# An RWKV-7 operand stage rewritten: scan over the raw tanh, key scale inside other operations, one factor on ScalarE

## The chip, the cores and the metric

The kernel runs on 1 core of a Trainium2 chip. The metric is the device time of one launch in microseconds (us), from runs of the same program; the time before is the median of 3 runs.

Engines are named as in the profile: PE (TensorE matmul), PEld (its weight load), DVE (VectorE), ACT (ScalarE), POOL (GpSimd), SP (SyncE, which issues most DMAs). Each works through its own instructions in order and waits for the others by semaphores.

## The reference, cut to what matters

A decoder trunk of two layers on 1024 tokens of width 1024. Layer 0 is an S5 diagonal SSM beside differential attention; layer 1 is RWKV-7 time mixing with 16 heads of 64; each is followed by a SwiGLU FFN of 2816 hidden columns. The change touches the operands of the RWKV-7 recurrence only:

```python
w = -softplus(-(w0 + tanh(xw @ w1) @ w2)) - 0.5
decay = exp(-exp(w))
k = xk @ w_k
a = sigmoid(a0 + (xa @ a1) @ a2)                 # learning rate, one per channel
kk = k * k_k
kk = kk / max(sqrt(sum(kk * kk, per head)), 1e-12)
k = k * (1.0 + (a - 1.0) * k_a)
# state: S_t = S_{t-1} diag(decay_t) + (S_{t-1} (-kk_t)) (kk_t*a_t)^T + v_t k_t^T;  y_t = S_t r_t
```

With a sigmoid written as 0.5 + 0.5 tanh(x/2), the log of the decay is -0.5 e^-0.5 (1 + tanh), and a is 0.5 (1 + tanh).

## The kernel before, in words

Dense products run on PE as three matmuls each (high and low parts of operands and weights, line 466), 128x512 a piece. Every weight block is loaded by DMA, rounded by ACT (`whi`, line 449) and its remainder taken by DVE or, in the stretches below, by POOL (`wlo`, line 450).

The recurrence is done in blocks of 512 tokens (two), each with 16 units: 8 pairs of heads times 2 pieces of 256 tokens. `rwkv_algebra` runs 19 steps per block. In a step four generators advance in lockstep on four successive units: `rwkv_prep` (operands, lines 1429 to 1496), `rwkv_inv` (a triangular inverse, built up in five rounds of small matmuls, lines 1566 to 1625), `rwkv_rec` (the recurrence over four chunks of 64 tokens, lines 1649 to 1676) and `rwkv_out`. Between their yields the matmuls of a dense product (FFN or projection) are woven in, so PE has work while the small chains pass through other engines. The order of PE's instructions is the order of the program text (`manual_schedule` for PE alone); the order on DVE, ACT, POOL and SP is set by a scheduler when the program is built.

Per unit `rwkv_prep` makes on [128 x 256] tiles: the log decay `lwt` (tanh on ACT, an affine on DVE, line 1430), its running sum `L` (four scans of 64, line 1432), `Wx` and `Wi` (exp of L and of -L, ACT), the learning rate `at` (tanh on ACT, affine on DVE, line 1445), the scaled key `kr` (DVE, 1447) and its square (ACT), the inverse root per head (`head_rsqrt`, which ends in a PE product `hbc`), then `kk` (DVE, 1453), `bt` (POOL, 1455, in the tile named `ksq`), the key factor `fk` (DVE, 1457, in the tile named `kr`), `k2` (DVE, 1459, in the tile named `lwt`), the four quarters of `FS` (bt and k2 times Wi, line 1464), and `AR` (kk times Wx on 1468, r times Wx on 1469). POOL makes `RV` = r times k2 (1470) and `FE` (1545).

In `rwkv_rec` each chunk is a chain of PE and DVE: PE `pR` (1649), DVE copy `Pb` (1655), PE `pR` (1659), copies `XU` (ACT 1660, DVE 1661), PE `pR` (1665), DVE state update `XH` (1672), and PE 1649 of the next chunk.

Of the kernel before, what the change touches and what calls it, by code (L numbers as in the profile page):

```python
# [12 lines left out]
AF = mybir.ActivationFunctionType  # L13
ALU = mybir.AluOpType
# [4 lines left out]
P = 128  # L19
# [18 lines left out]
EXPMH = math.exp(-0.5)  # L38
# [108 lines left out]
class Trunk:  # L147
# [1100 lines left out]
    def proj_open(self):  # L1248
        nc = self.nc
        v = nc.vector  # L1250
        vp = self.vp = self.open("m1v", 1)
        self.lastc = vp.tile([P, KT, 1], F32, name="m1lc")
        nc.gpsimd.memset(self.lastc, 0.0)
        vec = self.vec = vp.tile([P, 4, 8], F32, name="m1vec")
        o = self.v2
        v.tensor_scalar(vec[:, 0, :], self.vc2[:, o["od_w0"] : o["od_w0"] + 8], 0.5, None, op0=ALU.mult)
        v.tensor_scalar(vec[:, 1, :], self.vc2[:, o["od_a0"] : o["od_a0"] + 8], 0.5, None, op0=ALU.mult)
        v.tensor_scalar(vec[:, 2, :], self.vc2[:, o["od_k_a"] : o["od_k_a"] + 8], -1.0, 1.0, op0=ALU.mult, op1=ALU.add)
        self.omu = vp.tile([P, 48], F32, name="omu")
        v.tensor_scalar(self.omu, self.vc2[:, o["od_mu"] : o["od_mu"] + 48], -1.0, 1.0, op0=ALU.mult, op1=ALU.add)  # L1260

        self.tw, self.ta = (vp.tile([P, TB], F32, name=f"lt{i}") for i in "wa")
        nc.gpsimd.memset(self.tw[64:128, :], 0.0)
        nc.gpsimd.memset(self.ta[0:64, :], 0.0)
        self.sg = vp.tile([P, TB], F32, name="lsg")
        self.kd = self.dr.tile([3, 8, P, S], F32, name="kd")
        self.zd = self.dr.tile([8, P, S], F32, name="zd")
# [132 lines left out]
    def rwkv_prep(self, q, j, st):  # L1400


        nc = self.nc
        ap, pr, vec = self.ap, self.pr, self.vec
        v, g_, s_ = nc.vector, nc.gpsimd, nc.scalar
        sl = slice(j * P, (j + 1) * P)
        tok = slice(q * TR, (q + 1) * TR)
        tw, ta = (a[:, (q * TR) % TB : (q * TR) % TB + TR] for a in (self.tw, self.ta))
        M = ALU.mult
        rows = (slice(0, 64), slice(64, 128))  # L1410

        def t(tag, bufs=1, shape=None):
            return ap.tile(shape or [P, TR], F32, tag=tag, name=self.nm(tag), bufs=bufs)

        def c8(a):
            return a.rearrange("p (c t) -> p c t", t=64)

        ks, rr, RV = t("ks", 2), t("rr", 2), t("RV", 4, [P, 2, TR])
        for d, dst in ((0, ks), (1, rr), (2, RV[:, 1, :])):
            nc.sync.dma_start(dst, self.kd[d, j][:, tok])  # L1420
        wa2 = t("wa2", 2, [P, P])
        nc.sync.dma_start(wa2[0:64, :], self.A["od_w2"][0][:, sl])
        nc.sync.dma_start(wa2[64:128, :], self.A["od_a2"][0][:, sl])
        pz = pr.tile([P, TR], F32, tag="k", name=self.nm("pz"))
        nc.tensor.matmul(pz, lhsT=wa2, rhs=tw, start=True, stop=True)
        yield

        lwt, L = t("lwt"), t("L")
        s_.activation(lwt, pz, AF.Tanh, bias=vec[:, 0, j : j + 1], scale=0.5)
        v.tensor_scalar(lwt, lwt, -0.5 * EXPMH, -0.5 * EXPMH, op0=M, op1=ALU.add)  # L1430
        for c in range(0, TR, 64):
            v.tensor_tensor_scan(
                L[:, c : c + 64], self.ones[:, 0:1].to_broadcast([P, 64]), lwt[:, c : c + 64], 0.0, op0=M, op1=ALU.add
            )
        Wx = t("Wx", 1, [P, CR, 65])
        g_.memset(Wx[:, :, 0:1], 1.0)
        s_.activation(Wx[:, :, 1:65], c8(L), AF.Exp)
        Wi = L
        s_.activation(Wi, L, AF.Exp, scale=-1.0)
        pa = pr.tile([P, TR], F32, tag="k", name=self.nm("pa"))  # L1440
        nc.tensor.matmul(pa, lhsT=wa2, rhs=ta, start=True, stop=True)
        yield
        at = t("at")
        s_.activation(at, pa, AF.Tanh, bias=vec[:, 1, j : j + 1], scale=0.5)
        v.tensor_scalar(at, at, 0.5, 0.5, op0=M, op1=ALU.add)
        kr, ksq = t("kr"), t("ksq")
        v.tensor_scalar(kr, ks, self.col("od_k_k", j), None, op0=M)
        s_.activation(ksq, kr, AF.Square)
        yield
        rn = yield from self.head_rsqrt(ap, pr, "k", ksq, 1.0, None, 1e-24, TR // P)  # L1450
        yield
        kk = t("kk")
        v.tensor_tensor(kk, kr, rn, op=M)
        bt = t("ksq")
        g_.tensor_tensor(bt, kk, at, op=M)
        fk = t("kr")
        v.tensor_scalar(fk, at, self.col("od_k_a", j), vec[:, 2, j : j + 1], op0=M, op1=ALU.add)  # L1457
        k2 = t("lwt")
        v.tensor_tensor(k2, ks, fk, op=M)
        FS = t("FS", 2, [P, CR, P])  # L1460
        for h in range(2):
            r = rows[h]
            for x, o in ((bt, 64 * h), (k2, 64 - 64 * h)):
                v.tensor_tensor(FS[r, :, o : o + 64], c8(x)[r], c8(Wi)[r], op=M)  # L1464
        AR = [t(f"AR{h}", 3, [P, CR, P]) for h in range(2)]
        for h in range(2):
            r = rows[h]
            v.scalar_tensor_tensor(AR[h][r, :, 0:64], c8(kk)[r], -1.0, Wx[r, :, 0:64], op0=M, op1=M)  # L1468
            v.tensor_tensor(AR[h][r, :, 64:128], c8(rr)[r], Wx[r, :, 1:65], op=M)
        g_.tensor_tensor(RV[:, 0, :], rr, k2, op=M)  # L1470
        wc = t("wc", 3, [P, CR])
        g_.tensor_copy(wc, Wx[:, :, 64])
        st["pre"] = AR, FS, RV, wc
        yield

        XH, XU = ([t(f"{k}{h}", 3, [P, CR, 64]) for h in range(2)] for k in ("XH", "XU"))
        pv = pr.tile([P, CR, 64], F32, tag="k", name=self.nm("pv"))
        for c in range(CR):
            for h in range(2):
                nc.tensor.matmul(  # L1480
                    pv[rows[1 - h], c, :], lhsT=RV[rows[h], 1, c * 64 : (c + 1) * 64], rhs=self.cst("cen")[rows[h]], start=True, stop=True
                )
        for h in range(2):
            s_.copy(XH[h][rows[1 - h]], pv[rows[1 - h]])
            s_.copy(XU[h][rows[1 - h]], pv[rows[1 - h]])
        yield

        AB = t("AB", 3, [P, CR, P])
        msk = self.cst("tri").rearrange("p (o n) -> p o n", o=1)
        pas = [pr.tile([P, CR, P], F32, tag=g, name=self.nm("pA")) for g in "ky"]  # L1490
        for c in range(CR):
            for h in range(2):
                nc.tensor.matmul(pas[h][:, c, :], lhsT=FS[rows[h], c, :], rhs=AR[h][rows[h], c, :], start=True, stop=True)  # L1493
        for h, pa in enumerate(pas):
            for r, dst in ((rows[h], AB), (rows[1 - h], AR[h])):
                v.tensor_tensor(dst[r], pa[r], msk[r].to_broadcast([64, CR, P]), op=M)
            yield
        st["val"] = XH, XU, AB
# [364 lines left out]
```

## Time and profile before

| | |
|---|---|
| median of 3 runs | 3262.19 us (3261.68 to 3269.7) |
| profiled execution, its own time | 3254.43 us |
| its span in the trace | 3252.6 us |
| PE busy | 3020.0 us, 93% of the span |
| DVE busy | 1988.2 us, 61% |
| ACT busy | 1135.6 us, 35% |
| POOL busy | 913.8 us, 28% |
| mean granted TensorE clock | 0.964 |

A busy share is an average over stages with different limits. The two recurrence blocks lie at about 1190 to 1790 us and 2090 to 2690 us of the span. The profiled execution is one run of the program; it lies 7.8 us below the median of the runs. A granted clock of 1.00 is 2.4 GHz, one of 0.50 is 1.2 GHz.

### The profile page before, as it was taken

The page shows a single profiled execution, that of the slowest core. Times are in us where ns is not written, and L with a number is a line of the kernel's source. Part 1 is how long each engine was busy: PE and PEld are TensorE (multiplying, and loading weights), DVE is VectorE, ACT ScalarE, POOL GpSimd, SP SyncE. Part 2 cuts the span into 40 slices and gives each one's busy share as a digit, 9 for nine tenths or more (in the row PEclk, how much of TensorE's full clock was granted, in tenths as well). Part 3 has the DMA queues.
Part 4 walks back from the last instruction along what each step waited for, and adds up shares of the span by engine and source line. Part 5 has one row for each costly group of instructions (what it writes and reads, how often), then busy time and mean ns, then how long its engine had stood idle before and what let it go on. Part 6 is the DMA issues. An engine that isn't in the chain of part 4 may idle for free. (4 is left out here: it accounts for less than half of the span.)

```text
span 3252.6 us, 52003 instructions
## 1 busy us (share of the span) xinstructions
PE 3020.0 (93%) x19966; PEld 2255.1 (69%) x19966; DVE 1988.2 (61%) x4013; ACT 1135.6 (35%) x2286; POOL 913.8 (28%) x1034
## 2 busy tenths in 40 slices
PE   5789999998999999999899999999999999999999
PEld 2678866776777676666666776666666667777777
DVE  7754655556665556777777456467777774444443
ACT  3212443333224543333333246433333332322222
POOL 6643310001103103443433441034434334300000
PEclk7889998999999999999999999999999999999999
DMA  7753221226555441221221254422212212533333
GB/s 250 220 118 68 72 79 46 80 72 194 183 167 162 142 137 58 66 74 58 79 66 55 80 171 130 149 61 68 74 53 83 69 53 80 170 89 93 97 101 94
DMA packets 489864, 338.47 MB, mean 104 GB/s; under 512 B 44280, under 2 KB 451088, under 8 KB 488592
## 3 DMA queue, kind: packets, MB, share of 16 engines
q1 hardware_dynamic: 474288, 304.75, 31.2%
q0 software_dynamic: 7632, 25.64, 2.5%
q10 hardware_dynamic: 7696, 4.74, 0.6%
q8 instruction: 159, 2.61, 0.3%
q14 instruction: 89, 0.73, 0.1%
HBM read 292.59 MB, written 42.47 MB: 103 GB/s over the span
## 5 line engine op out<-in xcount | busy, mean ns | idle before, releaser
L449 ACT CAST whi<-wraw 128x1024 fp32r<-128x1024 f32 (+2 forms) x472 | 401.8, 852 | 896.3 <-PE pd L466 186.4
L466 PE MATMUL pd<-dd,whi 128*128 128x512 f32 x1408 | 464.0, 411 | 16.3 <-DVE x L534 12.2
L450 POOL TENSOR_TENSOR wlo<-wraw,whi 128x1024 fp32r<-128x1024 f32 (+2 forms) x184 | 326.6, 1776 | 483.1 <-ACT whi L449 403.1
L450 DVE TENSOR_TENSOR wlo<-wraw,whi 128x1024 fp32r<-128x1024 f32 (+2 forms) x288 | 297.4, 1033 | 264.0 <-ACT whi L449 252.3
L466 PE MATMUL pg<-fhi,whi 128*128 128x512 f32 x704 | 304.9, 433 | 13.2 <-DVE sg L521 10.8
L466 PEld LDWEIGHTS pd<-dd,whi 128*128 128x128 f32 x1408 | 253.4, 189 | 83.3 <-ACT whi L449 16.3
L466 PE MATMUL pu<-fhi,whi 128*128 128x512 f32 x704 | 298.8, 424 | 1.3 <-ACT ev L1359 0.6
L466 PE MATMUL pg<-fhi,wlo 128*128 128x512 f32 x704 | 284.9, 405 | 6.3 <-DVE wlo L450 6.3
L466 PE MATMUL pu<-fhi,wlo 128*128 128x512 f32 x704 | 281.6, 400 | 4.0 <-POOL wlo L450 2.4
L466 PE MATMUL pg<-flo,whi 128*128 128x512 f32 x704 | 283.4, 403 | 0.0
L466 PE MATMUL pd<-dd,wlo 128*128 128x512 f32 x704 | 279.2, 397 | 2.6 <-DVE wlo L450 2.1
L466 PE MATMUL pu<-flo,whi 128*128 128x512 f32 x704 | 280.8, 399 | 0.0
L534 DVE SCALAR_TENSOR_TENSOR x<-pd,mod,x 128x512 f32<-128x512 f32 x192 | 143.4, 747 | 125.3 <-PE pd L466 124.3
L466 PE MATMUL pkrv<-xh,whi 128*128 128x512 f32 x384 | 163.7, 426 | 12.5 <-ACT ev L1359 6.8
L466 PEld LDWEIGHTS pg<-fhi,whi 128*128 128x128 f32 x704 | 136.4, 194 | 49.0 <-DVE sg L521 11.9
L466 PEld LDWEIGHTS pg<-fhi,wlo 128*128 128x128 f32 x704 | 136.2, 193 | 40.6 <-DVE wlo L450 8.7
L466 PEld LDWEIGHTS pd<-dd,wlo 128*128 128x128 f32 x704 | 133.2, 189 | 39.2 <-DVE wlo L450 6.4
L466 PEld LDWEIGHTS pu<-fhi,whi 128*128 128x128 f32 x704 | 133.9, 190 | 37.8 <-issue 3.0
L466 PEld LDWEIGHTS pu<-fhi,wlo 128*128 128x128 f32 x704 | 134.5, 191 | 36.6 <-POOL wlo L450 3.3
L466 PE MATMUL pkrv<-xh,wlo 128*128 128x512 f32 x384 | 153.2, 399 | 2.5 <-DVE wlo L450 2.5
L466 PEld LDWEIGHTS pg<-flo,whi 128*128 128x128 f32 x704 | 137.0, 195 | 25.4
L466 PEld LDWEIGHTS pu<-flo,whi 128*128 128x128 f32 x704 | 134.9, 192 | 25.7
(459 smaller groups left out, 6116.0 us busy)
## 6 DMA issues: line engine op xcount, KB each, us to landing
wraw<-in_ffn_w_gate SPq DMA_DIRECT2D x88, 512.0 KB, 3.8
wraw<-in_ffn_w_up SPq DMA_DIRECT2D x88, 512.0 KB, 3.8
wraw<-in_ffn_w_down SPq DMA_DIRECT2D x128, 256.0 KB, 2.6
mwt<-in_w_ada POOLq DMA_DIRECT2D x48, 512.0 KB, 5.3
mwt<-in_w_ada SPq DMA_DIRECT2D x32, 512.0 KB, 5.8
wraw<-in_ffn_w_down SPq DMA_DIRECT2D x64, 192.0 KB, 2.3
kd<-ev SPq DMA_DIRECT2D x48, 256.0 KB, 2.0
xs<-x SPq DMA_DIRECT2D x8, 1024.0 KB, 5.6
```

The costliest lines, as they stand in the source:

```text
L449: nc.scalar.copy(hi, raw)
L450: (eng or nc.vector).tensor_tensor(lo, raw, hi.bitcast(F32), op=ALU.subtract)
L466: nc.tensor.matmul(out, lhsT=w(k), rhs=x(k), start=first and i == 0, stop=last and i == n - 1)
L534: nc.vector.scalar_tensor_tensor(x[:, n, :], pd, gate[:, n : n + 1], x[:, n, :], op0=ALU.mult, op1=ALU.add)
```

## The change

What it does, per unit of `rwkv_prep` (one more column group of constants, 0.5 k_a, is made once in `proj_open`):

- The affine on `lwt` goes. The scan's first operation becomes an add of the ones, so it sums 1 + tanh; the factor -0.5 e^-0.5 moves into the scale of the two exps.
- The affine on `at` goes: `at` stays the raw tanh. `bt` becomes (at + 1) times kk, on DVE (it was on POOL), and the missing 0.5 is put into the product with Wi (`FS`), which becomes a SCALAR_TENSOR_TENSOR.
- `kr` = k times k_k goes: the square takes k_k as ACT's scale, `kk` takes it as the scalar of a SCALAR_TENSOR_TENSOR.
- `fk` moves from DVE to ACT, with scale 0.5 k_a and bias 1 - 0.5 k_a.

```diff
@@ -1255,7 +1255,8 @@
         o = self.v2
         v.tensor_scalar(vec[:, 0, :], self.vc2[:, o["od_w0"] : o["od_w0"] + 8], 0.5, None, op0=ALU.mult)
         v.tensor_scalar(vec[:, 1, :], self.vc2[:, o["od_a0"] : o["od_a0"] + 8], 0.5, None, op0=ALU.mult)
-        v.tensor_scalar(vec[:, 2, :], self.vc2[:, o["od_k_a"] : o["od_k_a"] + 8], -1.0, 1.0, op0=ALU.mult, op1=ALU.add)
+        v.tensor_scalar(vec[:, 2, :], self.vc2[:, o["od_k_a"] : o["od_k_a"] + 8], -0.5, 1.0, op0=ALU.mult, op1=ALU.add)
+        v.tensor_scalar(vec[:, 3, :], self.vc2[:, o["od_k_a"] : o["od_k_a"] + 8], 0.5, None, op0=ALU.mult)
         self.omu = vp.tile([P, 48], F32, name="omu")
         v.tensor_scalar(self.omu, self.vc2[:, o["od_mu"] : o["od_mu"] + 48], -1.0, 1.0, op0=ALU.mult, op1=ALU.add)
 
@@ -1427,41 +1428,39 @@
 
         lwt, L = t("lwt"), t("L")
         s_.activation(lwt, pz, AF.Tanh, bias=vec[:, 0, j : j + 1], scale=0.5)
-        v.tensor_scalar(lwt, lwt, -0.5 * EXPMH, -0.5 * EXPMH, op0=M, op1=ALU.add)
         for c in range(0, TR, 64):
             v.tensor_tensor_scan(
-                L[:, c : c + 64], self.ones[:, 0:1].to_broadcast([P, 64]), lwt[:, c : c + 64], 0.0, op0=M, op1=ALU.add
+                L[:, c : c + 64], self.ones[:, 0:1].to_broadcast([P, 64]), lwt[:, c : c + 64], 0.0, op0=ALU.add, op1=ALU.add
             )
         Wx = t("Wx", 1, [P, CR, 65])
         g_.memset(Wx[:, :, 0:1], 1.0)
-        s_.activation(Wx[:, :, 1:65], c8(L), AF.Exp)
+        s_.activation(Wx[:, :, 1:65], c8(L), AF.Exp, scale=-0.5 * EXPMH)
         Wi = L
-        s_.activation(Wi, L, AF.Exp, scale=-1.0)
+        s_.activation(Wi, L, AF.Exp, scale=0.5 * EXPMH)
         pa = pr.tile([P, TR], F32, tag="k", name=self.nm("pa"))
         nc.tensor.matmul(pa, lhsT=wa2, rhs=ta, start=True, stop=True)
         yield
         at = t("at")
         s_.activation(at, pa, AF.Tanh, bias=vec[:, 1, j : j + 1], scale=0.5)
-        v.tensor_scalar(at, at, 0.5, 0.5, op0=M, op1=ALU.add)
-        kr, ksq = t("kr"), t("ksq")
-        v.tensor_scalar(kr, ks, self.col("od_k_k", j), None, op0=M)
-        s_.activation(ksq, kr, AF.Square)
+        ksq = t("ksq")
+        s_.activation(ksq, ks, AF.Square, scale=self.col("od_k_k", j))
         yield
         rn = yield from self.head_rsqrt(ap, pr, "k", ksq, 1.0, None, 1e-24, TR // P)
         yield
         kk = t("kk")
-        v.tensor_tensor(kk, kr, rn, op=M)
+        v.scalar_tensor_tensor(kk, ks, self.col("od_k_k", j), rn, op0=M, op1=M)
+
         bt = t("ksq")
-        g_.tensor_tensor(bt, kk, at, op=M)
+        v.scalar_tensor_tensor(bt, at, 1.0, kk, op0=ALU.add, op1=M)
         fk = t("kr")
-        v.tensor_scalar(fk, at, self.col("od_k_a", j), vec[:, 2, j : j + 1], op0=M, op1=ALU.add)
+        s_.activation(fk, at, AF.Identity, bias=vec[:, 2, j : j + 1], scale=vec[:, 3, j : j + 1])
         k2 = t("lwt")
         v.tensor_tensor(k2, ks, fk, op=M)
         FS = t("FS", 2, [P, CR, P])
         for h in range(2):
             r = rows[h]
             for x, o in ((bt, 64 * h), (k2, 64 - 64 * h)):
-                v.tensor_tensor(FS[r, :, o : o + 64], c8(x)[r], c8(Wi)[r], op=M)
+                v.scalar_tensor_tensor(FS[r, :, o : o + 64], c8(x)[r], 0.5 if x is bt else 1.0, c8(Wi)[r], op0=M, op1=M)
         AR = [t(f"AR{h}", 3, [P, CR, P]) for h in range(2)]
         for h in range(2):
             r = rows[h]
```

PE's instructions stand in the same order as before. In line numbers the functions behind the change are one lower. The scheduler places other engines' work anew; three places follow, all of the eighth unit of the first block unless said otherwise.

DVE, from `kk` on (the burst that follows the inverse root), before (`ksq` as a source is bt, `kr` is fk, `lwt` is k2):

```order
L1453 TENSOR_TENSOR kk_13607<-kr_13454,hbc_13582 128x256
L1575 TENSOR_TENSOR XE_13580<-X_13354,cstt 128x256
L1457 TENSOR_SCALAR kr_13611<-at_13451,vc_103,m1vec 128x256
L1468 SCALAR_TENSOR_TENSOR AR_2908_13620<-kk_13607,Wx_13415 64x4x64
L1468 SCALAR_TENSOR_TENSOR AR_2909_13621<-kk_13607,Wx_13415 64x4x64
L1459 TENSOR_TENSOR lwt_13613<-ks_13361,kr_13611 128x256
L1464 TENSOR_TENSOR FS_13615<-ksq_13609,L_13408 64x4x64 x2
L1661 COPY XU_2677_12747<-pR_13591 64x64
L1586 TENSOR_TENSOR QE_13605<-pA_13600,cstt 128x256
L1464 TENSOR_TENSOR FS_13615<-lwt_13613,L_13408 64x4x64 x2
L1447 TENSOR_SCALAR kr_13895<-ks_13802,vc_103 128x256
```

and now:

```order
L1451 SCALAR_TENSOR_TENSOR kk_13576<-ks_13334,vc_103,hbc_13551 128x256
L1574 TENSOR_TENSOR XE_13549<-X_13327,cstt 128x256
L1454 SCALAR_TENSOR_TENSOR ksq_13578<-at_13423,kk_13576 128x256
L1467 SCALAR_TENSOR_TENSOR AR_2900_13589<-kk_13576,Wx_13387 64x4x64
L1467 SCALAR_TENSOR_TENSOR AR_2901_13590<-kk_13576,Wx_13387 64x4x64
L1463 SCALAR_TENSOR_TENSOR FS_13584<-ksq_13578,L_13381 64x4x64 x2
L1660 COPY XU_2671_12724<-pR_13560 64x64
```

fk, k2 and the pair of FS made from k2 have left the burst, as has the next unit's `kr`; bt has come in.

DVE, the place in the same unit where the learning rate was formed, two recurrence chunks earlier, before:

```order
L1469 TENSOR_TENSOR AR_2908_13620<-rr_13362,Wx_13415 64x4x64
L1469 TENSOR_TENSOR AR_2909_13621<-rr_13362,Wx_13415 64x4x64
L1661 COPY XU_2677_12747<-pR_13391 64x64
L1445 TENSOR_SCALAR at_13451<-at_13451 128x256
L1672 SCALAR_TENSOR_TENSOR XH_2674_12744<-XH_2674_12744,wc_12716,pR_13429 64x64
L1672 SCALAR_TENSOR_TENSOR XH_2675_12745<-XH_2675_12745,wc_12716,pR_13429 64x64
L1591 TENSOR_TENSOR X_13354<-X_13354,pA_13436 128x32x2
L1575 TENSOR_TENSOR XE_13449<-X_13354,cstt 128x256
```

and now:

```order
L1468 TENSOR_TENSOR AR_2900_13589<-rr_13335,Wx_13387 64x4x64
L1468 TENSOR_TENSOR AR_2901_13590<-rr_13335,Wx_13387 64x4x64
L1660 COPY XU_2671_12724<-pR_13364 64x64
L1585 TENSOR_TENSOR QE_13378<-pA_13373,cstt 128x256
L1458 TENSOR_TENSOR lwt_13582<-ks_13334,kr_13580 128x256
L1671 SCALAR_TENSOR_TENSOR XH_2668_12721<-XH_2668_12721,wc_12693,pR_13401 64x64
L1671 SCALAR_TENSOR_TENSOR XH_2669_12722<-XH_2669_12722,wc_12693,pR_13401 64x64
L1463 SCALAR_TENSOR_TENSOR FS_13584<-lwt_13582,L_13381 64x4x64 x2
L1590 TENSOR_TENSOR X_13327<-X_13327,pA_13408 128x32x2
L1574 TENSOR_TENSOR XE_13421<-X_13327,cstt 128x256
```

The affine on `at` is gone, and k2 and the pair of FS made from k2 stand around the state update `XH`, ahead of `X` and `XE` of the inverse.

POOL, from the second inverse root (`hre`) to `FE`, before:

```order
L1519 COPY hre_13524<-hrp_13493 128x256
L450 TENSOR_TENSOR wlo_13642<-wraw_13639,whi_13641 128x1024
L1695 TENSOR_SCALAR Brk_13779<-cstt,vc_103 128x128
L1708 TENSOR_TENSOR y_2885_13532<-y_2885_13532,yq_13340 128x256
L1455 TENSOR_TENSOR ksq_13609<-kk_13607,at_13451 128x256
L1436 MEMSET Wx_13856 128x4
L1470 TENSOR_TENSOR RV_13363<-rr_13362,lwt_13613 128x256
L450 TENSOR_TENSOR wlo_13764<-wraw_13761,whi_13763 128x1024
L1545 TENSOR_TENSOR FE_13791<-FS_13615,wc_13627 128x512
```

and now, beginning one root earlier:

```order
L1515 TENSOR_TENSOR hrp_13362<-hrs_13360,mhalf 128x4
L1518 COPY hre_13399<-hrp_13362 128x256
L1469 TENSOR_TENSOR RV_13336<-rr_13335,lwt_13582 128x256
L1515 TENSOR_TENSOR hrp_13462<-hrs_13460,mhalf 128x4
L1518 COPY hre_13493<-hrp_13462 128x256
L450 TENSOR_TENSOR wlo_13611<-wraw_13608,whi_13610 128x1024
L1694 TENSOR_SCALAR Brk_13748<-cstt,vc_103 128x128
L1707 TENSOR_TENSOR y_2877_13501<-y_2877_13501,yq_13313 128x256
L1436 MEMSET Wx_13824 128x4
L1544 TENSOR_TENSOR FE_13760<-FS_13584,wc_13596 128x512
```

bt (`ksq`) is gone from POOL, and `RV` has moved from the burst to the earlier place, between the two inverse roots.

## Rows read from the trace of the kernel before

**Rows 1.** The page, part 1: engines' busy time, share of the span, instructions.
```profile
PE 3020.0 (93%) x19966; PEld 2255.1 (69%) x19966; DVE 1988.2 (61%) x4013; ACT 1135.6 (35%) x2286; POOL 913.8 (28%) x1034
```

**Rows 2.** Waits of PE, whole kernel: us in total, times, longest us.
```profile
PE pR L1665 <- DVE XU L1661: 45.3, 42, 3.7
PE pR L1649 <- DVE XH L1672: 17.7, 12, 2.7
PE pA L1613 <- DVE XE L1600: 4.0, 7, 1.2
```

**Rows 3.** PE in the two recurrence stretches: us, busy (instructions), granted clock, DMA.
```profile
1190.00:1790.00 600.00, 553.19 (x4879) 0.96 0.23 68
2090.00:2690.00 600.00, 554.60 (x4882) 0.96 0.23 68
```

**Rows 4.** Timeline of DVE, one burst: start us, us, engine line op out<-in xcount [idle].
```profile
1464.68 0.42 DVE L1453 TENSOR_TENSOR kk<-kr,hbc 128x256 f32<-128x256 f32 x1
...
1465.35 0.84 DVE L1457 TENSOR_SCALAR kr<-at,vc,m1vec 128x256 f32<-128x256 f32 x1
1466.11 0.84 DVE L1468 SCALAR_TENSOR_TENSOR AR<-kk,Wx 64x256 f32<-64x256 f32 x2
1466.98 0.42 DVE L1459 TENSOR_TENSOR lwt<-ks,kr 128x256 f32<-128x256 f32 x1
1467.33 1.30 DVE L1464 TENSOR_TENSOR FS<-ksq,L 64x256 f32<-64x256 f32 x2
1468.66 0.23 DVE L1661 COPY XU<-pR 64x64 f32<-64x64 f32 x1
...
1469.26 2.49 DVE L1464 TENSOR_TENSOR FS<-lwt,L 64x256 f32<-64x256 f32 x2
1471.78 1.24 DVE L1447 TENSOR_SCALAR kr<-ks,vc 128x256 f32<-128x256 f32 x1
...
1473.54 0.56 DVE L1672 SCALAR_TENSOR_TENSOR XH<-XH,wc,pR 64x64 f32<-64x64 f32 x2
```

**Rows 5.** Timeline of POOL beside that burst.
```profile
1467.49 0.86 POOL L1470 TENSOR_TENSOR RV<-rr,lwt 128x256 f32<-128x256 f32 x1 [0.37 <-PE pu L466]
1468.68 2.36 POOL L450 TENSOR_TENSOR wlo<-wraw,whi 128x1024 fp32r<-128x1024 f32 x1 [0.33 <-ACT whi L449]
```

**Rows 6.** Timeline of PE: four of its waits for DVE.
```profile
1286.47 0.34 PE L1665 MATMUL pR<-XU,BE 128*64 128x64 f32 x4 [0.54 <-DVE XU L1661]
...
1468.94 0.34 PE L1665 MATMUL pR<-XU,BE 128*64 128x64 f32 x4 [0.55 <-DVE XU L1661]
...
1474.16 0.48 PE L1649 MATMUL pR<-XH,AR 128*64 128x64 f32 x4 [2.17 <-DVE XH L1672]
...
2673.86 0.34 PE L1665 MATMUL pR<-XU,BE 128*64 128x64 f32 x4 [0.55 <-DVE XU L1661]
```

**Rows 7.** PE behind the first block's longer waits, columns as in Rows 3.
```profile
1320.00:1370.00 50.00, 43.44 (x396) 0.90 0.22 65
1470.00:1520.00 50.00, 45.49 (x394) 0.90 0.14 41
1620.00:1670.00 50.00, 44.05 (x397) 0.90 0.17 51
1700.00:1710.00 10.00, 7.81 (x76) 0.83 0.30 94
```

**Rows 8.** Timeline of DVE and PE, the place where the moved products land.
```profile
1452.35 0.29 DVE L1445 TENSOR_SCALAR at<-at 128x256 f32<-128x256 f32 x1
...
1453.62 0.42 DVE L1575 TENSOR_TENSOR XE<-X,cstt 128x256 f32<-128x256 f32 x1
...
1455.77 0.32 PE L1583 MATMUL pA<-XE,AC 128*32 128x64 f32 x8
```

**Rows 9.** Groups by line and shape: xcount | busy us, mean ns | idle before.
```profile
L1464 DVE TENSOR_TENSOR FS<-lwt,L 64x256 f32<-64x256 f32 x64 | 47.4, 741 | 0.7
L1703 ACT ACTIVATE y<-y,vc 128x256 f32<-128x256 f32 x32 | 19.2, 601 | 1.4 <-DVE y L1702 1.4
```

## The prediction

> **What bounds the kernel now.** I read the page's engine line first: PE is busy for 3020.0 of 3252.6 us, 93%, with DVE next at 61% [rows 1]. So only what ends PE's waits, or changes PE's clock, is worth anything. Next I read PE's waits by releaser. Three groups belong to the recurrence: 45.3 us for the DVE copy `XU`, 17.7 us for the state update `XH`, 4.0 us for `XE`, together 67.0 us [rows 2]. PE's own order is fixed and full of woven-in dense matmuls, so each of these waits moves the end.
>
> Then the stretches. In both recurrence blocks the granted clock averages 0.96 [rows 3], so each loses about 0.04 x 600 = 24 us of PE's work to the lower level of 1.2 GHz, 48 us in all. Where it is lost: around the longer waits of the first block the mean is 0.90, 0.90, 0.90 and 0.83 [rows 7], that is 0.10 x 50 three times and 0.17 x 10, about 17 us of the block's 24. A long wait is therefore paid twice.
>
> Last, what makes DVE late. The burst in the timeline starts with `kk` at 1464.68, and DVE does everything that `kk` allows in one go; the copy `XU` comes at 1468.66 and the update `XH` at 1473.54 [rows 4]. PE waited 0.55 us for the first and 2.17 us for the second [rows 6]. Three entries of the burst are longer than their work. `fk` takes 0.84. The FS pair from bt takes 1.30, with `RV` running on POOL beside it, and the pair from k2 takes 2.49 and ends with POOL's `wlo` of 2.36 [rows 4, 5]. The undisturbed pair is 0.87 (the `AR` pair, from 1466.11 to 1466.98). So a DVE operation with both inputs in SBUF waits for a POOL one that began earlier.
>
> **The change part by part.**
>
> *The path to XU.* From `kk` to `XU` it is 3.98 us now (1464.68 to 1468.66). `fk` leaves (1465.35 to 1466.11, 0.76), k2 leaves (1466.98 to 1467.33, 0.35), and the 0.43 that `RV` adds to the FS pair leaves, since `RV` follows k2. bt comes in at the spacing of `kk` or k2, 0.35 [rows 4]. Net 0.76 + 0.35 + 0.43 - 0.35 = 1.19 us earlier. Of the 42 waits for `XU`, 24 come within 8 us of a `kk` (the first at 1286.47, the last at 2673.86 [rows 6]); they hold 28.8 us. Six of them are 2.3 to 3.7 us long, 17.4 together, and shrink by 1.19 each, to about 10; the other 18 are all shorter than 1.19 and go. Gain 28.8 - 10 = 18.8 us. The other waits for `XU`, behind scans and masks, stay.
>
> *The path to XH.* Besides the 1.19, the FS pair from k2 (0.87 undisturbed, 2.49 here) and the next unit's `kr` (1.24 here) leave [rows 4]: 1.19 + 0.87 = 2.1 us at least, and 4.9 in this burst. All 12 waits for `XH` come behind a burst; the longest is 2.7 [rows 2], and in those POOL had stretched the burst. I take all 17.7 us as gained. Of the 4.0 us for `XE`, which follows `XH`, I take 3.
>
> *The clock.* Of the 17 us in rows 7, the parts behind `XH` waits go (about 10), and those behind the long `XU` waits, which only shrink, go by a small part: 11 per block, 22 for both, since the second repeats the first [rows 3]. Bounds: nothing, if the shorter waits still bring the clock down, and 48.
>
> *What comes in earlier in the unit.* k2 (0.35) and its FS pair (0.87), with `RV` behind k2 on POOL and so another 0.43, now stand ahead of `X` and `XE`; the affine on `at` (0.29) leaves there: +1.36 us. Today `XE` ends at 1454.04 and PE takes it at 1455.77 [rows 8], a cover of 1.73 us. A weight remainder on POOL can fall on this pair as it did in the burst: the 64 instructions averaged 741 ns [rows 9] against the 0.42 of an undisturbed `AR`, 0.64 us per unit. 1.36 + 0.64 is 0.27 over the cover, some 8 us over 32 units. Stalls come in lumps, and a lump costs clock too, so I charge 14. Bounds: 0, if the cover always holds, and 93 (below, the rival on the slow side). Were the cover gone altogether, the 2.0 us would be paid in each unit, 64 us.
>
> *ACT.* `fk` with two per-partition operands is like `y`, 601 ns [rows 9], 19 us over 32 units on an engine that is 35% busy [rows 1]; the two waits it could add are for k2, which has the cover above. The square grows by no more than that 601 ns, and its result waits for PE's place in the order anyway. Bounds for both: 0 to 0.6 us per unit; I take 0. POOL loses 32 x bt and gains nothing. The scan keeps its shape, and the affine before it, of the shape of that on `at` (0.29), leaves a chain that ends in none of the three groups of rows 2; 0. The extra constant is one instruction on 8 columns; 0.
>
> *A rule against the change.* The `AR` pair is already a SCALAR_TENSOR_TENSOR with both sources in SBUF and takes 0.84 for two, 0.42 each, as the plain k2 does [rows 4]; so FS and bt are priced alike in either form. The Trainium skill ("Vector Engine (DVE) Microarchitecture Reference", Points that are easy to get wrong) says that this form with two non-bf16 SBUF sources runs at half throughput; the trace does not bear it out. By that rule bt and the four FS would double, which is the third rival.
>
> *The sum.* 18.8 + 17.7 + 3 + 22 - 14 = 47.5 us. Against the profiled execution's own 3254.4 that gives 3207. It ran 7.8 us under the median of the runs, 3262.2, so for the median I forecast **3215 us**.
>
> **The rivals.**
>
> 1. *The wait only moves: no change (within 0.3%, 9.8 us, about what a measurement of this kernel can tell from nothing).* The early pair eats the gain, or PE, no longer waiting for `XU`, waits a little later for what the weights need. For it: the new place lies ahead of the inverse, which PE also needs. Against it: the cover of 1.73 us. It needs 48 us more than I charge, or 1.5 us in each unit. Time 3262. Chance 10%.
>
> 2. *Slower: POOL's `wlo` falls on the early FS pair as a rule.* Then the pair takes 2.49 in place of 0.87, and the delay is 1.36 + 1.62 - 1.73 = 1.25 us per unit, 40 us, plus a fall of the clock each time at the 1.7 us that the shortest in rows 7 cost, 54 us: 93 together. Against gains of 61.5 that is 32 us slower, 3294. It decides from about 21 of the 32 units on. For it: the pair was hit so often that its mean is 741. Against it: POOL is busy 28% of the time [rows 1], and in the new order `RV` and the roots stand there. Chance 6%.
>
> 3. *The rewritten operations run at half speed (the rule above).* bt and the FS pair of the burst grow by 1.27 us, and the gain for `XU` is gone; the early pair grows by 0.85, 27 us. What is left is 17.7 + 1 + 11 - 14 - 27, 11 us slower: 3273. Chance 3%.
>
> 4. *More than forecast.* The early place costs nothing and the clock stays up throughout: 67 + 48 = 115 at most, 3147. Chance of a gain over 85 us: 6%.
>
> **How the numbers follow.** The forecast, a gain of 10 to 85 us, has 75%. With rival 4 that makes 0.81 for faster by over 0.3%; rival 1 gives 0.10 for no difference; rivals 2 and 3 give 0.09 for slower. The range 3177 to 3258 is the gain from 85 down to 4; it leaves out rival 4, most of the slow side and half of rival 1, some 2 in 10.
>
> **What would show it right or wrong.** Right: the waits of PE for `XU` near 26 us and for `XH` near 0; granted clock in the recurrence stretches 0.97 to 0.98; the FS pair from bt near 0.85 and no longer beside `RV`; the FS pair from k2 still above 422 ns each. DVE's busy time falls by more than 20 us (0.84 + 0.29 - 0.42 in each unit, with `kr` and the affine on `lwt` on top), and POOL loses a product per unit. Wrong: waits of PE for `X` or `XE` of the inverse (PE's small matmuls on 1578 and 1583 before the change) that were not there, or new long waits with the clock under 0.96. FS or bt near 0.84 each would make rival 3 right. If `XH` waits persist, the burst was not their cause.

## The result, and the profile after

The change ran at a median of 3192.08 us (four runs, 3185.14 to 3195.38) and the kernel before, beside it, at 3265.94 us (four runs, 3261.68 to 3273.81): a ratio of 0.977 [0.9754 to 0.9787], faster, and inside the range of 3177 to 3258. The gain between the medians is 74 us where 47.5 were forecast; run again later (told under experiment 4), the change gained 65 us over the kernel before that ran beside it.

The page of the changed kernel, engines' busy time, for [rows 1]:

```profile
PE 2998.9 (94%) x19966; PEld 2242.3 (70%) x19966; DVE 1940.1 (61%) x3918; ACT 1157.8 (36%) x2318; POOL 891.2 (28%) x1002
```

DVE loses 48.1 us of work, POOL 22.6, ACT gains 22.2. PE does the same 19966 instructions; its busy time falls by 21 us while the granted clock of the two blocks rises from 0.96 to 0.99 (below). That PE is still the bound is plain: its share of the span is now 94%.

PE's waits in the whole changed kernel (us in total, times, longest), those that the change touches, for [rows 2]:

```profile
PE pR L1664 <- DVE XU L1660: 24.2, 25, 2.5
...
PE pA L1582 <- DVE Pb L1654: 5.6, 10, 1.4
...
PE pA L1582 <- DVE XE L1574: 2.1, 3, 1.2
```

The waits for `XU` fell from 45.3 to 24.2 us; those for `XH` (17.7) and for the `XE` of line 1600 (4.0) have no row any more. A new row stands at PE's line 1582, put down to `Pb` and, as before, to `XE`.

The recurrence blocks of the changed kernel, PE alone (us, busy and instructions, granted clock, DMA), for [rows 3]:

```profile
1180.00:1750.00 570.00, 542.74 (x4873) 0.99 0.25 76
2060.00:2630.00 570.00, 547.01 (x4939) 0.99 0.24 71
```

About as many PE instructions as in [rows 3] now take 570 us instead of 600 in each block, and the granted clock is 0.99 where it was 0.96.

The burst of the unit that [rows 4] showed, DVE's timeline in the changed kernel (`ksq` as a source is bt):

```profile
1461.37 0.48 DVE L1451 SCALAR_TENSOR_TENSOR kk<-ks,vc,hbc 128x256 f32<-128x256 f32 x1
...
1462.11 0.42 DVE L1454 SCALAR_TENSOR_TENSOR ksq<-at,kk 128x256 f32<-128x256 f32 x1
1462.44 0.84 DVE L1467 SCALAR_TENSOR_TENSOR AR<-kk,Wx 64x256 f32<-64x256 f32 x2
1463.32 0.85 DVE L1463 SCALAR_TENSOR_TENSOR FS<-ksq,L 64x256 f32<-64x256 f32 x2
1464.20 0.23 DVE L1660 COPY XU<-pR 64x64 f32<-64x64 f32 x1
...
1465.40 0.57 DVE L1671 SCALAR_TENSOR_TENSOR XH<-XH,wc,pR 64x64 f32<-64x64 f32 x2
```

From `kk` to `XU` it is 2.83 us instead of 3.98, and from `kk` to `XH` 4.03 instead of 8.86. PE's row just behind, `pR` on the copy, carries no wait:

```profile
1465.01 0.34 PE L1664 MATMUL pR<-XU,BE 128*64 128x64 f32 x4
```

And the early place of the same unit, for [rows 8], DVE with `k2` (`lwt`) and the FS pair made from it, then POOL's `RV` beside them:

```profile
1449.42 0.59 DVE L1458 TENSOR_TENSOR lwt<-ks,kr 128x256 f32<-128x256 f32 x1
1449.93 0.57 DVE L1671 SCALAR_TENSOR_TENSOR XH<-XH,wc,pR 64x64 f32<-64x64 f32 x2
1450.53 1.01 DVE L1463 SCALAR_TENSOR_TENSOR FS<-lwt,L 64x256 f32<-64x256 f32 x2
1451.56 0.22 DVE L1590 TENSOR_TENSOR X<-X,pA 128x64 f32<-128x64 f32 x1
1451.82 0.43 DVE L1574 TENSOR_TENSOR XE<-X,cstt 128x256 f32<-128x256 f32 x1
```

```profile
1450.09 0.73 POOL L1469 TENSOR_TENSOR RV<-rr,lwt 128x256 f32<-128x256 f32 x1 [0.36 <-DVE lwt L1458]
```

`XE` ends at 1452.25. PE takes it at 1452.45 with no wait: the cover of 1.73 us of [rows 8] is nearly used up here, but not overdrawn.

**Where the time came from.** I measure the stage from the first sigmoid of the gate to the last store of the result: 1606.0 us before (1162.1 to 2768.1), 1535.8 after (1166.8 to 2702.6), a difference of 70.2. What lies ahead grew by 4.7 us and what lies behind by 5.1 in the two profiled executions; the change does not touch either. The clock accounts for both: summed over windows of 10 us as below, it costs 64.9 us ahead of the stage before and 69.9 after, and 0.6 and 6.7 behind it. In the second profile of the same change it costs 61.2 us ahead, so several us of it come and go from one execution to the next without any edit. Two sums explain the stage. The first is PE's waits for the recurrence's tiles (XU, XH, XE, X, QE, Pb, all rows of the view of waits that name them). The second is the clock: over every 10 us of the two blocks, 10 times (1 minus the granted clock).

| | PE's waits, us | clock, us (windows under 0.97) | sum | stage |
|---|---|---|---|---|
| before | 71.1 | 45.9 (25) | 117.0 | 1606.0 |
| after | 32.9 | 13.6 (6) | 46.5 | 1535.8 |
| difference | 38.2 | 32.3 | 70.5 | 70.2 |

The difference of the sums is that of the stage, to within 0.3 us. The same table over all the kernels of this study is at the end of the experiments; what a kernel saves in the sum is nowhere more than 5 us from what it saves in the stage. Each row rests on one profiled execution.

### The profile page after: what moved, and what is told of

It reads as the page before. It is cut to its first block, busy times and chain, and to the rows that moved or that the text cites. A ratio compares the mean times of both kernels' runs of the same rounds, so it can differ in the third digit from the quotient of the medians.

```text
span 3192.2 us, 51849 instructions
## 1 busy us (share of the span) xinstructions
PE 2998.9 (94%) x19966; PEld 2242.3 (70%) x19966; DVE 1940.1 (61%) x3918; ACT 1157.8 (36%) x2318; POOL 891.2 (28%) x1002
## 5 line engine op out<-in xcount | busy, mean ns | idle before, releaser
L466 PE MATMUL pd<-dd,whi 128*128 128x512 f32 x1408 | 463.3, 410 | 12.8 <-DVE x L534 7.8
L466 PE MATMUL pkrv<-xl,whi 128*128 128x512 f32 x384 | 153.1, 399 | 0.0
```

The lines of the kernel that those rows point to most:

```text
L466: nc.tensor.matmul(out, lhsT=w(k), rhs=x(k), start=first and i == 0, stop=last and i == n - 1)
```

## The experiments

Why could `fk`, `k2` and half of `FS` leave the burst? None of them needs the root. The order listed ahead of the prediction shows that they left, not why. The code says it: every tile of `rwkv_prep` has one buffer unless a number is given,

```python
def t(tag, bufs=1, shape=None):
    return ap.tile(shape or [P, TR], F32, tag=tag, name=self.nm(tag), bufs=bufs)
```

and before the change `fk` was made in the tile named `kr`, which held `kr` until `kk` had read it, behind the root. Once `kr` is no longer formed, the tile is free early.

**Theory A:** the gain comes from the free tile. It lets `fk`, `k2`, `RV` and an FS pair run ahead of the root, the burst shortens, and PE's waits and clock falls go with it. **Theory B,** the rival: the gain comes from the work that is saved on DVE and POOL or moved off them, whatever the order. **Theory C,** a second rival: one of the other edits (bt off POOL, the factor on ACT) makes the gain by itself. The ratio of each experiment is to the kernel before that ran beside it: 3251.32 us for experiments 1 to 4, 3256.22 for 5, 6 and the change run again.

**1. The order alone, all the work kept.** The kernel before; `fk` gets a tile that is free at that point, and two statements move ahead of the root.

```diff
         v.tensor_scalar(at, at, 0.5, 0.5, op0=M, op1=ALU.add)
+        fk = t("kk")
+        v.tensor_scalar(fk, at, self.col("od_k_a", j), vec[:, 2, j : j + 1], op0=M, op1=ALU.add)
+        k2 = t("lwt")
+        v.tensor_tensor(k2, ks, fk, op=M)
...
-        fk = t("kr")
-        v.tensor_scalar(fk, at, self.col("od_k_a", j), vec[:, 2, j : j + 1], op0=M, op1=ALU.add)
-        k2 = t("lwt")
-        v.tensor_tensor(k2, ks, fk, op=M)
```

Expected:

> The kernel before, with one thing changed: fk takes the tile of kk instead of that of kr, and fk and k2 are written ahead of the root, so that fk, k2 and the FS pair made from k2 (and RV on POOL) stand early, as in the change. All the work is the old work: both affines, kr, fk on DVE, bt on POOL. Theory A (the burst's length sets PE's waits): k2's FS pair, k2 and fk leave the burst, kr stays in it and bt stays on POOL beside AR. XU is 0.76 + 0.35 + 0.43 = 1.5 us earlier less 0.3 for kr; most of the waits for XH go. Ratio to before 0.980 to 0.985 (gain 50 to 65 us), waits of PE for XU 25 to 32 us, for XH under 4. Theory B (the saved DVE and POOL work is what counts, wherever it stands): no work is saved, so ratio 0.997 to 1.003.

Measured: 3199.93 us (3195.99 to 3207.99) against 3251.32 of the kernel before, 0.9852 [0.9822 to 0.9883]. The engines and PE's waits in this kernel:

```profile
PE 2991.6 (94%) x19966; PEld 2237.2 (70%) x19966; DVE 1987.8 (62%) x4013; ACT 1136.5 (36%) x2286; POOL 915.5 (29%) x1034
```

```profile
PE pR L1665 <- DVE XU L1661: 27.0, 26, 3.1
...
PE pA L1583 <- DVE Pb L1655: 9.7, 12, 1.5
...
PE pR L1649 <- DVE XH L1672: 2.1, 2, 1.0
```

DVE does the 4013 instructions and 1988 us of before, POOL its 1034: no work is saved. Yet `XU` falls to 27.0, `XH` to 2.1, and the stage to 1551.1 us, 54.9 of the 70.2. As the main cause, Theory B falls here; the 15 us that are missing in the stage are left for it.

**2. The change with `kr` formed again.** All other edits stay; the tile is taken again.

```diff
-        ksq = t("ksq")
-        s_.activation(ksq, ks, AF.Square, scale=self.col("od_k_k", j))
+        kr, ksq = t("kr"), t("ksq")
+        v.tensor_scalar(kr, ks, self.col("od_k_k", j), None, op0=M)
+        s_.activation(ksq, kr, AF.Square)
...
-        v.scalar_tensor_tensor(kk, ks, self.col("od_k_k", j), rn, op0=M, op1=M)
+        v.tensor_tensor(kk, kr, rn, op=M)
```

Expected:

> The change, with the key scale undone: kr is formed on DVE again, squared and multiplied by the root. fk, still on ACT, again takes kr's tile, which kk reads, so fk, k2, RV and both FS pairs fall back into the burst. The affines, bt on DVE and fk on ACT stay as in the change. Theory A: XU only 0.76 - 0.35 = 0.4 us earlier than before, XH the same with kr and the FS pair ahead of it: gain 10 to 25 us of the 74, ratio to before 0.992 to 0.997; waits for XU 32 to 40 us, for XH 10 to 16. Theory B: of the saved DVE work of some 1.4 us a unit 1.1 remain: gain 50 to 60 us, ratio 0.982 to 0.985.

Measured: 3236.87 us (ten runs, 3230.06 to 3263.97), 0.9964 [0.9943 to 0.9986]; four fifths of the gain are lost. PE's waits in this kernel, then DVE's timeline in the burst of the same unit, then POOL's beside it:

```profile
PE pR L1665 <- DVE XU L1661: 32.9, 33, 2.8
PE pR L1649 <- DVE XH L1672: 20.3, 13, 2.6
...
PE pA L1613 <- DVE XE L1600: 3.8, 6, 1.2
```

```profile
1483.05 0.42 DVE L1452 TENSOR_TENSOR kk<-kr,hbc 128x256 f32<-128x256 f32 x1
...
1484.94 0.42 DVE L1459 TENSOR_TENSOR lwt<-ks,kr 128x256 f32<-128x256 f32 x1
1485.28 1.29 DVE L1464 SCALAR_TENSOR_TENSOR FS<-ksq,L 64x256 f32<-64x256 f32 x2
1486.61 0.23 DVE L1661 COPY XU<-pR 64x64 f32<-64x64 f32 x1
...
1487.21 2.91 DVE L1464 SCALAR_TENSOR_TENSOR FS<-lwt,L 64x256 f32<-64x256 f32 x2
1490.15 1.24 DVE L1446 TENSOR_SCALAR kr<-ks,vc 128x256 f32<-128x256 f32 x1
...
1491.91 0.56 DVE L1672 SCALAR_TENSOR_TENSOR XH<-XH,wc,pR 64x64 f32<-64x64 f32 x2
```

```profile
1485.44 0.85 POOL L1470 TENSOR_TENSOR RV<-rr,lwt 128x256 f32<-128x256 f32 x1 [0.37 <-DVE lwt L1459]
1487.04 2.37 POOL L450 TENSOR_TENSOR wlo<-wraw,whi 128x1024 fp32r<-128x1024 f32 x1 [0.75 <-ACT whi L449]
```

The old burst is back: `k2` behind `kk`, `RV` beside the first FS pair (1.29), `wlo` beside the second (2.91), and `XH` at 8.86 us behind `kk`, the very distance of [rows 4]. `XU` is 3.56 behind `kk` instead of 3.98, since `fk` is on ACT and bt has come in; that is what the rest of the edits is worth there, and it shows in `XU` (32.9 against 45.3) and not in `XH` (20.3 against 17.7; the expectation of 10 to 16 was missed). The profiled execution was the longest of the ten, 3263.97 us; it differs ahead of the stage, where the clock cost 87.0 us against 64.9. Its stage of 1593.2 us is 12.8 below that of the kernel before, close to the 14 between the medians. Order alone (54.9) and the other edits without the order (12.8) make 67.7 of the 70.2 us together.

**3. The change with the learning rate formed again:** the affine on `at` comes back to DVE, bt to POOL, FS takes a factor of 1.0, the constants of `fk` are adapted.

```diff
+        v.tensor_scalar(at, at, 0.5, 0.5, op0=M, op1=ALU.add)
...
-        v.scalar_tensor_tensor(bt, at, 1.0, kk, op0=ALU.add, op1=M)
+        g_.tensor_tensor(bt, kk, at, op=M)
```

Expected:

> The change, with the learning rate formed again: the affine on at is back on DVE, bt is a plain product on POOL, FS has no factor. The rest as in the change. Theory A: the burst loses bt (0.35) but AR can wait for bt on POOL (0.4); the affine of 0.3 stands early, under the cover. Within 8 us of the change: ratio to before 0.975 to 0.980. Theory B: a third of the saved work is back and the contention of bt on POOL too: 20 to 30 us slower than the change, ratio 0.984 to 0.987.

Measured: 3191.38 us (3189.32 to 3195.05), 0.9824 [0.9797 to 0.9851].

**4. The change with the factor on DVE:**

```diff
-        s_.activation(fk, at, AF.Identity, bias=vec[:, 2, j : j + 1], scale=vec[:, 3, j : j + 1])
+        v.tensor_scalar(fk, at, vec[:, 3, j : j + 1], vec[:, 2, j : j + 1], op0=M, op1=ALU.add)
```

Expected:

> The change, with fk on DVE again, as one TENSOR_SCALAR on the raw tanh; it still stands early, with k2 behind it. Theory A: the early place is longer by 0.3 to 0.4 us (fk alone, without bt beside it) less the wait for ACT, of a cover of 1.7: 0 to 8 us slower than the change, ratio to before 0.977 to 0.980. Theory B: 0.4 to 0.8 us of DVE work a unit is back: 13 to 26 us slower than the change, ratio 0.981 to 0.985.

Measured: 3186.21 us (3181.67 to 3200.77), 0.9815 [0.9779 to 0.9851]. Neither ratio lies where Theory A put it: that of experiment 3 is above its range and below Theory B's, that of experiment 4 lies in Theory B's, and the interval of experiment 3 lies above that of the change's first runs. But those ranges were set by the change's first ratio, and the change itself, run again beside experiment 6,

> The change itself, as the yardstick of the runs beside it. Ratio to before 0.975 to 0.982, as in its first runs and as the earlier experiments lay.

gave 3191.15 us, 0.9806 [0.9777 to 0.9834], and the three intervals overlap in most of their length; against the kernels before beside them, experiments 3 and 4 and the change run again gain 60, 65 and 65 us. Neither forming the rate (with bt on POOL) nor the engine of the factor makes a difference that these runs can tell. Theory C falls for these two edits.

**5. The change with `kr` formed again, but `fk` in a tile that is free.** The work of experiment 2 with the tile of experiment 1. Beside the tile, only the place of two statements in the text differs from experiment 2, and that place alone can't be the cause: in the change they stand where experiment 2 has them, and `fk` leaves the burst all the same.

```diff
+        fk = t("kk")
+        s_.activation(fk, at, AF.Identity, bias=vec[:, 2, j : j + 1], scale=vec[:, 3, j : j + 1])
+        k2 = t("lwt")
+        v.tensor_tensor(k2, ks, fk, op=M)
+        kr, ksq = t("kr"), t("ksq")
+        v.tensor_scalar(kr, ks, self.col("od_k_k", j), None, op0=M)
+        s_.activation(ksq, kr, AF.Square)
```

(The later statements for `fk` and `k2` go, and `kk` is `kr` times the root, as in experiment 2.) Expected:

> As the run in which kr was formed again, but fk takes kk's tile and fk and k2 are written ahead of the root: kr is formed on DVE in every unit, in the burst, and yet fk, k2, RV and k2's FS pair can stand early. Theory A (what counts is that the shared tile no longer holds fk back; the work of kr is small change): within 12 us of the change, slower by the 0.3 us that kr adds to the burst ahead of XU in some units, so ratio to the change 1.000 to 1.004, waits for XU 24 to 29 us, for XH under 3. Theory B (kr's own work made that run slow): no better than that run, 40 us or more slower than the change.

Measured: 3187.11 us (3182.7 to 3188.75), 0.9788 [0.9763 to 0.9812]: the change's time, with the operations of experiment 2, whose ratio is 0.9964. PE waits 23.2 us for `XU` and not at all for `XH`. Forming `kr` costs nothing that can be told; `fk` having to wait for its tile cost four fifths of the gain. Theory A stands.

**6. The change with the last copy `XU` on ACT.** What is left of the waits for `XU` comes from DVE being late, and ACT already makes the other of the two copies.

```diff
-            v.tensor_copy(XU[1][rows[1], c, :], pu[rows[1], :])
+            s_.copy(XU[1][rows[1], c, :], pu[rows[1], :])
```

Expected:

> The change, and beside it the second half of XU is copied by ACT instead of DVE, so PE no longer waits for a copy that stands behind a burst, masks or a stalled product on DVE. If the waits that are left for XU on DVE (24 us, and some of the clock that falls behind them) are all paid on PE: 20 to 35 us faster than the change, waits for XU on DVE gone. If ACT's own queue takes their place (casts of 1.05 us, y of 0.6 ahead of the copies, and two copies of 0.2 in a row): within 8 us of the change, with waits of PE 1664 for ACT.

Measured: 3162.28 us (3160.22 to 3168.78), 0.9717 [0.9691 to 0.9742], 28.9 under the change that ran beside it; it beats both kernels. Its PE has no row for `XU` from DVE any more, nor one for line 1664 from ACT. The largest rows that are left are those of the early place and of the inverse, each longer than in the change:

```profile
PE pA L1582 <- DVE Pb L1654: 8.0, 17, 1.5
...
PE pA L1589 <- DVE QE L1585: 4.0, 4, 1.2
PE pA L1582 <- DVE XE L1574: 3.7, 5, 1.7
```

**The account of all kernels,** with the two sums as in the section on the result:

| kernel | PE's waits | clock (windows) | sum | stage | saved: sum, stage | gain of the medians |
|---|---|---|---|---|---|---|
| before | 71.1 | 45.9 (25) | 117.0 | 1606.0 | | |
| 2, `kr` formed again | 61.6 | 39.1 (22) | 100.7 | 1593.2 | 16.3, 12.8 | 14 |
| 1, order alone | 43.7 | 17.0 (11) | 60.7 | 1551.1 | 56.3, 54.9 | 51 |
| 4, factor on DVE | 35.5 | 23.8 (12) | 59.3 | 1544.0 | 57.7, 62.0 | 65 |
| 3, rate formed again | 32.5 | 15.3 (9) | 47.8 | 1540.5 | 69.2, 65.5 | 60 |
| the change | 32.9 | 13.6 (6) | 46.5 | 1535.8 | 70.5, 70.2 | 74 |
| 5, `kr` and a free tile | 30.5 | 15.3 (10) | 45.8 | 1535.5 | 71.2, 70.5 | 69 |
| the change again | 31.0 | 11.9 (8) | 42.9 | 1533.0 | 74.1, 73.0 | 65 |
| 6, `XU` on ACT | 17.8 | 5.1 (3) | 22.9 | 1511.5 | 94.1, 94.5 | 94 |

Two quantities that the trace gives directly, PE's waits and its clock, hold it to within 5 us, although DVE's work differs by 82 us between experiments 1 and 6.

## Why the prediction came out right, point by point

**The bound.** PE's waits in the recurrence and PE's clock were named as the only things worth anything. The account bears it out to within 5 us in every kernel.

**XU, 18.8 forecast:** 21.1 measured. The mechanism is borne out unit by unit. Of the 24 units whose waits were counted, the path from `kk` to `XU` shortened by 1.13 to 1.23 us in 20 (forecast 1.19) and by 1.82 in two; in two it did not, since DVE there has the FS pair from bt ahead of the copy now and had it behind before. Near `kk` 9.5 us of waits are left where 10 were forecast, six longer ones and the 0.2 us of these two units. The other waits, behind scans and masks, fell from 16.5 to 14.7. The two longest that are left come from `wlo` on the burst, and did so before: there it held the `AR` pair of that unit, now it holds the FS pair from bt, which elsewhere takes 0.85. DVE's, POOL's and PE's rows of one of these units before:

```profile
1356.85 2.94 DVE L1468 SCALAR_TENSOR_TENSOR AR<-kk,Wx 64x256 f32<-64x256 f32 x2
```

```profile
1357.05 2.46 POOL L450 TENSOR_TENSOR wlo<-wraw,whi 128x1024 fp32r<-128x1024 f32 x1 [0.27 <-ACT whi L449]
```

```profile
1362.80 0.48 PE L1665 MATMUL pR<-XU,BE 128*64 128x64 f32 x4 [3.67 <-DVE XU L1661]
```

and in the changed kernel, where the wait is 1.13 us shorter:

```profile
1358.98 2.94 DVE L1463 SCALAR_TENSOR_TENSOR FS<-ksq,L 64x256 f32<-64x256 f32 x2
...
1363.00 0.23 DVE L1660 COPY XU<-pR 64x64 f32<-64x64 f32 x1
```

```profile
1358.67 2.53 POOL L450 TENSOR_TENSOR wlo<-wraw,whi 128x1024 fp32r<-128x1024 f32 x1 [4.32 <-ACT whi L449]
```

```profile
1363.28 0.34 PE L1664 MATMUL pR<-XU,BE 128*64 128x64 f32 x4 [2.54 <-DVE XU L1660]
```

**XH 17.7 and XE 3 forecast:** 17.7 and 4.0. Both rows are gone; experiment 2, which brings the burst back, brings them back (20.3 and 3.8). The burst was their cause. The 4.9 us named for the burst of [rows 4] came out as 4.83 (from 8.86 to 4.03).

**What stretched the burst** was read a little too narrowly. The FS pair from k2 did not end with `wlo` but 0.7 us behind it (1471.75 and 1471.04 in [rows 4, 5]). Nor was it only operations with both inputs in SBUF: `fk`, with the one tensor `at` and per-partition scalars, took 0.84 us, with bt running on POOL from 1465.18 for 0.86; its shortest is 0.40. The prices were read from the rows and are not touched by that.

**The early place, a charge of 14:** 6.5, that is 5.6 for `Pb` and 0.9 more for `XE`. The step assumed that `wlo` would stretch the early FS pair as it had in the burst, by 0.64 per unit over what is undisturbed. It did not: the groups by line and shape (times, then min/median/max in ns, first and last start) show the pair from k2 in the kernel before, then in the change:

```profile
L1464 DVE TENSOR_TENSOR FS<-lwt,L x64: 405/422/2518, 1217.8 to 2676.2; 64x256 f32<-64x256 f32 x64
```

```profile
L1463 DVE SCALAR_TENSOR_TENSOR FS<-lwt,L x64: 409/423/930, 1193.8 to 2595.5; 64x256 f32<-64x256 f32 x64
```

The longest is 930 ns instead of 2518, the mean 565 instead of 741 [rows 9]. Where it is longer than 423 in the units shown, `RV`, which follows k2 on POOL, runs beside it. What the early place does cost can be followed in the first unit of this kind, on DVE, POOL and PE:

```profile
1271.37 2.48 DVE L1432 TENSOR_TENSOR_SCAN L<-ones,lwt 128x64 f32<-128x64 f32 x1
...
1276.55 0.42 DVE L1458 TENSOR_TENSOR lwt<-ks,kr 128x256 f32<-128x256 f32 x1
1277.00 0.22 DVE L1590 TENSOR_TENSOR X<-X,pA 128x64 f32<-128x64 f32 x1
1277.14 1.35 DVE L1463 SCALAR_TENSOR_TENSOR FS<-lwt,L 64x256 f32<-64x256 f32 x2
1278.53 0.43 DVE L1574 TENSOR_TENSOR XE<-X,cstt 128x256 f32<-128x256 f32 x1
1278.87 0.22 DVE L1654 COPY Pb<-pR 128x64 f32<-128x64 f32 x1
```

```profile
1271.32 2.38 POOL L450 TENSOR_TENSOR wlo<-wraw,whi 128x1024 fp32r<-128x1024 f32 x1 [4.76 <-ACT whi L449]
...
1277.05 0.73 POOL L1469 TENSOR_TENSOR RV<-rr,lwt 128x256 f32<-128x256 f32 x1 [2.51 <-DVE lwt L1458]
```

```profile
1279.10 0.32 PE L1582 MATMUL pA<-XE,AC 128*32 128x64 f32 x8 [1.45 <-DVE Pb L1654]
```

A scan beside `wlo` makes DVE late; k2 then stands ahead of `X` and the FS pair between `X` and `XE`, and PE waits 1.45 us. The matmul reads `XE`, which ended at 1278.96; the row names `Pb`, which ended at 1279.09. Which of the two released PE can't be told from the row, but the same entries push both back. This is the first rival's mechanism, in some ten waits and far from the 1.5 us per unit that it needed. None of the six windows with a lowered clock holds one of these waits, so the clock that the charge allowed for was not paid. The second rival's needed `wlo` on the pair in 21 units; with no instruction over 930 ns, it fell on none in full.

**The clock, 22 forecast:** 32.3. This is the step that was mis-sized most. It took 17 us of a block's 24 as lying behind long waits, left most of what lay behind the `XU` waits that only shrink as lost, and gave nothing for the falls outside [rows 7]. Measured, 25 windows with a lowered clock became 6, in the first block 13 became 2; so the falls outside [rows 7] mostly went too. 32.3 lies inside the stated bounds of 0 and 48; several us of it may be the execution's own, as the stretches outside the stage show.

**ACT, 0 forecast:** `fk` takes 600 ns on ACT, and k2 waits for it ten times, 9.5 us in all; no row of PE's waits names it. The square with its scale takes 508 ns, 418 before. Experiment 4, with `fk` on DVE, has the same time as far as it can be told. Zero was right as far as these runs can tell.

**Half speed, the third rival:** the rewritten FS has a median of 423 ns, as the plain product had 422 (the two rows above); bt takes 419. The Trainium skill ("Vector Engine (DVE) Microarchitecture Reference", Points that are easy to get wrong) says that this form with two non-bf16 SBUF sources halves throughput. By an estimate from that it would take near twice as long; the trace does not agree.

**The sum.** 21.1 + 17.7 + 4.0 - 6.5 + 32.3 is 68.6, and 1.9 more in smaller rows. Forecast 47.5; of the 23 between, the clock is 10.3 and the early place 7.5. Both missed on the same side, so the total did not come out by errors that cancel. Of what was to be seen, `XU` near 26 is 24.2, `XH` is 0, the clock is 0.99 where 0.97 to 0.98 was named, DVE fell by 48 where over 20 was named, POOL lost its product. One thing named as a sign of being wrong came too, in small: the new waits on PE's line 1582, the 6.5 us of the early place.

**What the prediction did not name** is what let the work move. It read the new order from the listing and priced its two paths rightly, but took `kr` leaving as a small part of the path to `XH`, and the scale inside the square as worth nothing. By experiments 1, 2 and 5 that edit is most of the change: it frees the tile in which `fk` is made, and the order that follows is worth 54.9 of the 70.2 us by itself.

**Open.** Experiment 1 stays 15 us behind the change in the stage, and experiment 2 gives 12.8 for the other edits; which of them holds that remainder was not found. Experiments 3 and 4 stand 5 and 8 behind it by one profile each, too near the 2.8 between the two profiles of the change to settle the parts; the affine ahead of the scan was not undone by itself. Experiment 4 shows a clock loss of 23.8 us at PE's waits of 35.5, where the change has 13.6 at 32.9. Its profiled execution, 3200.77 us, was the longest of its four and 14.6 above their median, so that row overstates what the edit costs; why the clock fell more often in that execution was not found.

## What to carry to other kernels

Before counting what an edit saves, list which tile it gives back and who is waiting for that name: one buffer that is held across a long dependency (here an inverse root) pins everything that reuses it behind that dependency, and a free name for one small factor can be worth more than all the operations removed (54.9 us against 12.8 here). Price a move by the chain that ends a wait of the bound engine, and count a wait that disappears together with the clock that comes back behind it. Where short operations stay late on a busy engine, give them to the one that already makes their twin: one copy moved to ACT was worth another 28.9 us.

## What the runs showed of the hardware that was not expected

Equal waits did not lower the clock equally. In the changed kernel the wait of 2.54 us that ended at 1363.28 and one of 2.53 us on the same line that ended at 2222.72 stand in these windows (PE alone; the fourth value is the granted clock, after us, busy and instructions):

```profile
1360.00:1370.00 10.00, 7.46 (x85) 1.00 0.07 21
2220.00:2230.00 10.00, 7.47 (x68) 0.66 0.07 21
```

The busy share of the ten microseconds is the same, and one has a granted clock of 1.00, the other of 0.66. What tells them apart was not found, so in this kernel a single wait's share of the clock could not be told from its length; over a stage, the account above shows the two falling together.

The product `kk` on DVE, one source of which PE wrote in either form, rose from 420 to 480 ns when it took a per-partition scalar as well, while bt and FS, with a constant and both sources in SBUF, kept the duration of a plain product. On ACT a per-partition scale made the square of the same shape 508 ns instead of 418; `fk`, another function with a scale and a bias per partition, took 600.
